# A fused mixer and mixture-of-experts layer: the first norm's weight and bias applied to gathered rows instead of stored rows, and both norms' vectors spread in the router's tail

## The chip, the core and the metric

One core of one Trainium2 chip. The metric is device time of one execution in microseconds (us), smaller is better. The kernel is written with Bass and Tile; TensorE (PE in the profile), VectorE (DVE), ScalarE (ACT), GpSimd (POOL) and SyncE (SP, which only issues DMAs) run side by side, and semaphores hold them together.

## What is computed

One layer on 1024 tokens of width 1024: a mixer (two kinds of gated linear attention, not touched here), a residual and a norm, a router that picks one of 8 groups and 2 of its 8 experts for each token, the 64 experts, a residual and a second norm.

```python
def layer_norm(x, g, b):
    ...
    return ((xf - mu) * lax.rsqrt(var + LN_EPS) * g + b).astype(x.dtype)

h = hybrid_mixer(x, ...)                       # ends with o @ w_out
x = layer_norm(DEEPNORM_ALPHA * x + h, ln1_g, ln1_b)
h = hierarchical_moe(x, ...)                   # router, top 2 of 64 experts, gates
x = layer_norm(DEEPNORM_ALPHA * x + h, ln2_g, ln2_b)

# inside hierarchical_moe, for the rows xb_ of one expert e
h = jax.nn.silu(xb_ @ w_gate[e]) * (xb_ @ w_up[e])
return h @ w_down[e]
```

Each expert has three weight matrices of 1024x512, 512x1024 in f32, 2 MB each.

## The kernel before

The program has three stages. The **mixer** runs to about 480 us. The **router stage** loops over eight tiles of 128 tokens (L952 to 979): output projection (L858 to 860), residual and statistics of norm 1 on VectorE (L868 to 885), the normalised row on ScalarE (`scaled_rows`, L894), its weight and bias on GpSimd (L896, L897, on the whole row for tiles 0 to 6; on tile 7 VectorE takes 704 columns and GpSimd 320), a store of the row to the DRAM array `x1d` (L898), and beside that the router's logits (transposes L908, matmuls L916, into which norm 1's weight and bias are already folded), the choice of experts (L763 to 808, VectorE with small ScalarE exponentials), and each token's rank within its expert (`ranks`: matmuls L814, L815, L840, with VectorE's L821 to L829). The tables of which token stands in which row of which expert (`gidx`, `oidx`, `gcol`; L982 to 987) close the stage.

The **expert stage** (`pairs`, from L1139) walks over 32 pairs of experts; 64 rows of each expert make one tile of 128 rows. A pair has six weight units of 2 MB (gate, up and down of both experts) that the SP queue loads into eight slots (`load_unit`, L719 on; tiles `w1u`, `w2u`). A slot is loaded anew as soon as the matmuls that read it are done. For a pair the order on TensorE is: 32 gate and up matmuls (L1156, 64 records), the rows' sums of an earlier pair (`add_rows`, L1114), the transposes of the hidden units (L1040), the transposes of the next pair's rows (`transposed`, L1024), and 16 down matmuls (L1182, 32 records); this order is written out by hand, the other engines' orders are set by the scheduler. The rows come through GpSimd's indirect DMA: `gather` (L1010) reads a pair's 128 rows of `x1d` into one of four buffers `xgs`, two pairs ahead of use. Once a pair's sums are known, VectorE adds the residual, which are those same gathered rows, in place and applies norm 2 to them (`finish_rows` L1117, L1123 and L1124; the norm L1054 to 1057, with rsqrt steps L80 to L88), and `scatter` (L1015) writes them to the output. A token has two experts; a row's norm is taken where both parts are known, and the indices of the others point outside the array.

In pair 0 `spread_ln2` (L1074 to 1084) makes copies of norm 2's weight and bias on all 128 partitions: `ident` times the vector's columns on VectorE (L1078), four matmuls by a matrix of ones (L1082, eight records), and ScalarE copies to SBUF. The buffers `xgs`, two for transposed rows (`xts`) and the two vectors share `VOA`, eight tiles of 128x1024 that the mixer used before. After the pairs a loop over overflow blocks follows for experts with more than 64 rows; it is counted at run time.

Of the kernel before, what the change touches and what calls it, by code (L numbers as in the profile page):

```python
# [9 lines left out]
F32 = mybir.dt.float32  # L10
# [3 lines left out]
AF = mybir.ActivationFunctionType  # L14
OP = mybir.AluOpType
# [4 lines left out]
D = 1024  # L20
NT = T // 128
KT = D // 128
NH = 8
NE = 64
# [32 lines left out]
def mixer_moe_kernel(ctx: ExitStack, tc: tile.TileContext, x_in, xT_in, wf_in, wv_in, wvg_in, wa2_in,  # L57
                     cols_in, wout_in, ln_in, wr_in, wg_in, wu_in, wd_in, const_in, out):
    nc = tc.nc
    npair = NE // 2  # L60
    V, S, G, PE = nc.vector, nc.scalar, nc.gpsimd, nc.tensor
# [640 lines left out]
    rp = b1.enter_context(tc.tile_pool(name="rp", bufs=2, reuse_waits="tile"))  # L702
    sp2 = b1.enter_context(tc.tile_pool(name="sp2", bufs=2, reuse_waits="tile"))
    wout_tiles(rp, [7])
    lnb = rp.tile([128, 2, D], F32, name="lnb", bufs=1)
    wr = rp.tile([128, KT, 72], F32, name="wr", bufs=1)
    load_wout(7, rp, D)
    for i in range(2):
        S.dma_start(lnb[:, i], ln_in[i:i + 1].to_broadcast([128, D]))
    S.dma_start(wr, wr_in)  # L710
    w1p = ctx.enter_context(tc.tile_pool(name="w1", bufs=W1N, side="right", reuse_waits="tile"))
    units = []
# [175 lines left out]
    def scaled_rows(t):  # L888

        r = rt[t]  # L890
        rs, nm, _ = stats[t]
        for n in range(2):
            ns = slice(n * 512, (n + 1) * 512)
            S.activation(r[:, ns], r[:, ns], AF.Identity, bias=nm, scale=rs)  # L894
        for E, cs in ((G, slice(0, D)),) if t < NT - 1 else ((V, slice(0, 704)), (G, slice(704, D))):
            E.tensor_tensor(r[:, cs], r[:, cs], lnb[:, 0, cs], OP.mult)  # L896
            E.tensor_tensor(r[:, cs], r[:, cs], lnb[:, 1, cs], OP.add)  # L897
        S.dma_start(x1d[t * 128:(t + 1) * 128], r)  # L898

    def logits(t):  # L900
# [51 lines left out]
    for t in range(NT):  # L952
# [20 lines left out]
        if t:  # L973
            scaled_rows(t - 1)
    scaled_rows(t)
    router(t)
    for u in (t - 1, t):
        ranks(u, stats[t][2])
# [16 lines left out]
    ps_c = mp.enter_context(tc.tile_pool(name="ps_c", bufs=2, space=PSUM))  # L995
    w2p = ctx.enter_context(tc.tile_pool(name="w2", bufs=W2N, reuse_waits="tile"))
    m1 = ctx.enter_context(tc.tile_pool(name="m1", bufs=1, reuse_waits="tile"))

    room = [VOA[:, i].rearrange("p h d -> p (h d)") for i in range(NT)]
    xgs, xts = room[:4], room[6:]  # L1000
    ln2 = VOA[:, 4:6].rearrange("p a h d -> p a (h d)")
    for xg in xgs[:2]:
        G.memset(xg, 0.0)
    mw = ctx.enter_context(tc.tile_pool(name="mw", bufs=2, reuse_waits="tile"))
# [4 lines left out]
    def gather(dst, idx):  # L1009
        return G.indirect_dma_start(out=dst, out_offset=None, in_=x1d,  # L1010
                             in_offset=bass.IndirectOffsetOnAxis(ap=idx, axis=0),
                             bounds_check=T - 1, oob_is_err=False)
# [2 lines left out]
        return G.indirect_dma_start(out=dst, out_offset=bass.IndirectOffsetOnAxis(ap=idx, axis=0),  # L1015
                             in_=src, in_offset=None, bounds_check=rows - 1, oob_is_err=False)

    def transposed(src, i):
        xt = xts[i].rearrange("p (c s) -> p c s", c=KT)
        sv = src.rearrange("p (k c) -> p c k", c=KT)  # L1020
        for half in range(2):
            tp = ps_x.tile([128, 4, 128], F32, name="tp")
            for i in range(4):
                PE.transpose(tp[:, i], sv[:, half * 4 + i], ident)  # L1024
            S.copy(xt[:, 4 * half:4 * half + 4], tp)
        return xt

    def product(gp, up):
# [22 lines left out]
    def norm2(o, stats_of, w):  # L1051

        mv = mw.tile([128, 2], F32, name="mv")
        V.bn_aggr(mv, stats_of.rearrange("p a b -> p (a b)"))  # L1054
        rs = rstd_of(mw, mv[:, 1:2], 1, "z")
        V.scalar_tensor_tensor(o, o, mv[:, 0:1], w[:, 0], op0=OP.subtract, op1=OP.mult)
        return V.scalar_tensor_tensor(o, o, rs, w[:, 1], op0=OP.mult, op1=OP.add)  # L1057

    over = m1.tile([128, 1], I32, name="over")
    onum = m1.tile([128, 1], I32, name="onum")  # L1060
# [10 lines left out]

    one1 = m1.tile([128, 1], F32, name="one1")

    def spread_ln2():  # L1074

        w = xgs[3]
        for i in range(2):
            V.tensor_tensor(w.rearrange("p (q c) -> p q c", c=8), ident[:, :, None].to_broadcast([128, 128, 8]),  # L1078
                            cols[:, None, 50 + 8 * i:58 + 8 * i].to_broadcast([128, 128, 8]), OP.mult)
            for n in range(2):  # L1080
                cp = ps_c.tile([128, 512], F32, name="cp")
                PE.matmul(cp, one1.to_broadcast([128, 128]), w[:, n * 512:(n + 1) * 512], start=True, stop=True)  # L1082
                S.copy(ln2[:, i, n * 512:(n + 1) * 512], cp)
        G.memset(w, 0.0)

    GP = 4

# [28 lines left out]

    def finish_rows(p, cps):  # L1117

        xg = xgs[p % 4]
        st = mw.tile([128, 2, 6], F32, name="st")  # L1120
        for n in range(2):
            ns = slice(n * 512, (n + 1) * 512)
            V.scalar_tensor_tensor(xg[:, ns], xg[:, ns], ALPHA, cps[n], op0=OP.mult, op1=OP.add)  # L1123
            V.bn_stats(st[:, n], xg[:, ns])  # L1124
        norm2(xg, st, ln2)
        outs.append(scatter(out, oidx[:, p:p + 1], xg, T))

    ys, outs = {}, []
    for p in range(2):
        g = gather(xgs[p], gidx[:, p:p + 1])  # L1130
        if p == 0:
            first = g
    G.memset(one1, 1.0)
    G.memset(xgs[2], 0.0)
    why = "the rows of the first pair go before weights that are needed later"
# [3 lines left out]
    def pairs():  # L1139


        wm = ps_c.tile([128, 128], F32, name="cp")
        for i in range(8):

            PE.matmul(wm, ident, ident, start=True, stop=True)
        last = npair - 1
        xt, cps, ms, trow = transposed(xgs[0], 0), None, None, None
        for p in range(npair):
            if p + 2 < npair:
                gather(xgs[(p + 2) % 4], gidx[:, p + 2:p + 3])  # L1150
            gp = ps_g.tile([128, FF], F32, name="gu")
            up = ps_g.tile([128, FF], F32, name="gu")
            for u, dst in ((0, gp), (2, up)):
                for c in range(KT):
                    for b in range(2):
                        PE.matmul(dst[64 * b:64 * b + 64], xt[:, c, 64 * b:64 * b + 64], utile[6 * p + u + b][:, c],  # L1156
                                  start=(c == 0), stop=(c == KT - 1))
                for b in range(2):
                    load_unit(6 * p + u + b + W1N + W2N)
            sg = product(gp, up)  # L1160
            if p:
                cps = [ps_c.tile([128, 512], F32, name="cp") for _ in range(2)]
                add_rows(cps, ms)
            hT = hidden(sg)
            if p:
                finish_rows(p - 1, cps)
            if p == 0:
                spread_ln2()
            if p < last:
                xt = transposed(xgs[(p + 1) % 4], (p + 1) % 2)  # L1170
            if p % GP == 0:
                trow = group_rows(p // GP)
            ms = masks(trow, p)
            if p == last:
                cps = [ps_g.tile([128, 512], F32, name="gu") for _ in range(2)]
                add_rows(cps, ms[:-1], last=False)
            yps = [ps_y.tile([128, 512], F32, name="yp") for _ in range(2)]
            ys[p] = yring.tile([128, 2, D], F32R, name="y")
            for n in range(2):
# [16 lines left out]
    def block_tables():  # L1196
# [20 lines left out]
        blk = cst[:, C_BLK:C_BLK + NOV]  # L1217
        ex = t1(NOV)
        for q in range(NOV // 16):
            cm = xts[q % 2].rearrange("p (a b) -> p a b", b=NE)  # L1220
            V.tensor_tensor(cm, inc[:, None, :].to_broadcast([128, 16, NE]),
                            blk[:, 16 * q:16 * q + 16, None].to_broadcast([128, 16, NE]), OP.is_le)
            V.tensor_reduce(ex[:, 16 * q:16 * q + 16], cm, AX.X, OP.add)
# [33 lines left out]
    def block(i):  # L1257
# [6 lines left out]
        V.tensor_copy(oc, ogate[:, bass.ds(i, 1)])  # L1264
        xo = xgs[0]
        gather(xo, oi[:, 0:1])
        xt = transposed(xo, 0)
        gp = ps_g.tile([128, FF], F32, name="gu")
        up = ps_g.tile([128, FF], F32, name="gu")
        for src, dst in ((wg_in, gp), (wu_in, up)):  # L1270
# [16 lines left out]
    def block_sums():  # L1287
        for t in range(NT):
            z, y0, y1 = xgs[0], xgs[1], xgs[2]
            ts = slice(t * 128, (t + 1) * 128)  # L1290
            nc.sync.dma_start(z, x1d[ts])
            nc.sync.dma_start(y0, yd[ts])
            nc.sync.dma_start(y1, yd[T + t * 128:T + (t + 1) * 128])
            V.tensor_tensor(y0, y0, y1, OP.add)
# [76 lines left out]
```

## Time and profile before

| | us |
|---|---|
| median of 3 runs | 1600.44 |
| lowest, highest | 1598.53, 1600.70 |
| the profiled execution | 1601.88 |
| its span in the profile | 1600.1 |

| engine | busy us | share of the span | instructions |
|---|---|---|---|
| PE | 1442.8 | 90% | 9303 |
| DVE | 730.9 | 46% | 1842 |
| ACT | 408.1 | 26% | 752 |
| POOL | 276.8 | 17% | 228 |

The page gives one execution. [...] A timeline row gives start, duration, engine, line, operation, output and input tile, count, and in brackets the engine's idle time before it with what ended it. A row of the waits sums those idle times. An f32 matmul of the program leaves two records, a transpose one.

### The profile page before, as it was taken

Reading aid. Unit: us, or ns where it says so; the run is one execution under the profiler, and the core shown is the slowest. Engines: PE = TensorE matmul, PEld = TensorE weight load, DVE = VectorE, ACT = ScalarE, POOL = GpSimd, SP = SyncE. Lnnn points to the kernel's source line nnn. Section 1 sums busy time; section 2 is a strip of 40 time slices with the busy share of each in tenths; the row PEclk is TensorE's granted clock in tenths of the full one; section 3 lists DMA queues with packets and bytes.
Section 4 is the critical chain, followed back from the end, with each engine's and each line's share of the span. In section 5 each row is a group of like instructions: output and inputs, shape, how many; then the busy total and the mean of one; then the engine's idle time right before and its main releaser. Section 6 shows DMA issues by size and latency. Waiting matters only on the chain. (4 is left out here: it accounts for less than half of the span.)

```text
span 1600.1 us, 22873 instructions
## 1 busy us (share of the span) xinstructions
PE 1442.8 (90%) x9303; PEld 798.1 (50%) x9303; DVE 730.9 (46%) x1842; ACT 408.1 (26%) x752; POOL 276.8 (17%) x228
## 2 busy tenths in 40 slices
PE   7999999899999987999889899889988989889985
PEld 5777678677777873343333233334333334333432
DVE  4657645667768993242233234224223323422424
ACT  5545544555533222111111101101111110110110
POOL 4524223323204441000000000000100000000000
PEclk8999999999999997999999999999999999998998
DMA  4101111010137246999999999999999999999992
GB/s 166 42 27 35 34 34 34 29 34 27 35 105 317 80 179 260 398 426 427 425 426 427 426 427 426 426 425 426 426 426 426 426 425 427 425 425 426 420 391 87
DMA packets 61966, 450.18 MB, mean 281 GB/s; under 512 B 12192, under 2 KB 20640, under 8 KB 36896
## 3 DMA queue, kind: packets, MB, share of 16 engines
q1 hardware_dynamic: 50768, 430.01, 64.7%
q0 software_dynamic: 9216, 12.61, 2.2%
q10 hardware_dynamic: 1872, 6.06, 1.0%
q8 instruction: 74, 1.21, 0.3%
q14 instruction: 36, 0.29, 0.1%
HBM read 448.63 MB, written 20.97 MB: 293 GB/s over the span
## 5 line engine op out<-in xcount | busy, mean ns | idle before, releaser
L1156 PE MATMUL gu<-w2u,VOA 128*64 128x512 f32 x1024 | 261.3, 639 | 45.4 <-DMA w2u<-in_wu_dram 28.4
L1156 PE MATMUL gu<-w1u,VOA 128*64 128x512 f32 x1024 | 259.8, 626 | 32.1 <-DMA w1u<-in_wu_dram 23.2
L1032 DVE TENSOR_TENSOR sg<-sg,gu 128x512 f32<-128x512 f32 x32 | 22.0, 687 | 542.8 <-PE gu L1156 542.8
L1156 PEld LDWEIGHTS gu<-w2u,VOA 128*64 128x64 f32 x1024 | 80.6, 147 | 215.3 <-issue 151.4
L1156 PEld LDWEIGHTS gu<-w1u,VOA 128*64 128x64 f32 x1024 | 82.5, 143 | 204.7 <-issue 152.7
L176 PE MATMUL pp<-xh,wh 128*128 128x512 f32 x416 | 173.1, 416 | 0.0
L178 PE MATMUL pp<-xl,wh 128*128 128x512 f32 x416 | 166.0, 399 | 0.0
L180 PE MATMUL pp<-xh,wl 128*128 128x512 f32 x416 | 165.0, 397 | 0.0
L1015 POOL DMA_INDIRECT out_dram<-VOA,oidx x32 | 32.2, 1005 | 604.7 <-DVE VOA L1057 592.9
L1042 ACT COPY hT<-tp 128x512 f32<-128x512 f32 x32 | 18.7, 585 | 386.4 <-PE tp L1040 386.4
L1182 PE MATMUL yp<-w1u,hT 128*64 128x512 f32 x512 | 117.2, 595 | 0.0
L1182 PE MATMUL yp<-w2u,hT 128*64 128x512 f32 x512 | 113.4, 595 | 0.0
L1048 ACT ACTIVATE y<-yp,gcol 128x512 fp32r<-128x512 f32 x64 | 44.0, 687 | 191.2 <-PE yp L1182 191.2
L176 PEld LDWEIGHTS pp<-xh,wh 128*128 128x128 f32 x416 | 79.0, 190 | 18.4 <-issue 1.9
L180 PEld LDWEIGHTS pp<-xh,wl 128*128 128x128 f32 x416 | 79.1, 190 | 17.3
L471 POOL TENSOR_TENSOR d<-P 128x512 f32<-128x512 f32 x36 | 51.6, 1433 | 202.3 <-DVE ny L88 65.3
L178 PEld LDWEIGHTS pp<-xl,wh 128*128 128x128 f32 x416 | 79.3, 191 | 13.7
L1010 POOL DMA_INDIRECT VOA<-x1d,gidx x32 | 32.7, 1021 | 292.6 <-issue 225.2
L1049 DVE SCALAR_TENSOR_TENSOR y<-yp,gcol,y 128x512 fp32r<-128x512 f32 x64 | 47.9, 749 | 77.4 <-ACT y L1048 77.1
L1031 ACT ACTIVATE sg<-gu 128x512 f32<-128x512 f32 x32 | 19.1, 597 | 246.7 <-PE gu L1156 246.7
L1114 PE MATMUL cp<-y,same 128*128 128x512 f32 x304 | 78.5, 404 | 0.0
L1114 PEld LDWEIGHTS cp<-y,same 128*128 128x128 f32 x304 | 54.7, 188 | 35.5 <-issue 25.2
(276 smaller groups left out, 2076.2 us busy)
## 6 DMA issues: line engine op xcount, KB each, us to landing
w1u<-in_wu_dram SPq DMA_DIRECT2D x32, 2048.0 KB, 29.5
w1u<-in_wd_dram SPq DMA_DIRECT2D x32, 2048.0 KB, 30.1
w2u<-in_wg_dram SPq DMA_DIRECT2D x31, 2048.0 KB, 26.8
w1u<-in_wg_dram SPq DMA_DIRECT2D x30, 2048.0 KB, 29.3
w2u<-in_wd_dram SPq DMA_DIRECT2D x30, 2048.0 KB, 30.4
w2u<-in_wu_dram SPq DMA_DIRECT2D x30, 2048.0 KB, 28.6
wr<-in_wf_dram SPq DMA_DIRECT2D x36, 256.0 KB, 2.6
r<-in_x_dram SPq DMA_DIRECT2D x8, 512.0 KB, 3.5
```

The source lines that it names most:

```text
L176: PE.matmul(ps, hi[:, k], xh[:, k, ts], start=(k == 0), stop=False)
L178: PE.matmul(ps, hi[:, k], xl[:, k, ts], start=False, stop=False)
L180: PE.matmul(ps, lo[:, k], xh[:, k, ts], start=False, stop=(k == KT - 1))
L471: G.tensor_tensor(ev[:, :, 0], ref, Pv[:, :, 0], OP.subtract)
L1010: return G.indirect_dma_start(out=dst, out_offset=None, in_=x1d, in_offset=bass.IndirectOffsetOnAxis(ap=idx, axis=0), bounds_check=T - 1, ...
L1015: return G.indirect_dma_start(out=dst, out_offset=bass.IndirectOffsetOnAxis(ap=idx, axis=0), in_=src, in_offset=None, bounds_check=rows - ...
L1032: V.tensor_tensor(sg, sg, up, OP.mult)
L1048: S.mul(yh[:, ns], yps[n], gate_col)
L1049: V.scalar_tensor_tensor(yl[:, ns], yps[n], gate_col, yh[:, ns], op0=OP.mult, op1=OP.subtract)
L1114: PE.matmul(cps[n], m, ys[q][:, i, n * 512:(n + 1) * 512], start=(first and j == 0 and i == 0), stop=(last and j == len(ms) - 1 and i == 1))
L1156: PE.matmul(dst[64 * b:64 * b + 64], xt[:, c, 64 * b:64 * b + 64], utile[6 * p + u + b][:, c], start=(c == 0), stop=(c == KT - 1))
L1182: PE.matmul(yps[n][64 * b:64 * b + 64], hT[:, c, 64 * b:64 * b + 64], utile[6 * p + 4 + b][:, c, n * 512:(n + 1) * 512], start=(c == 0), s ...
```

## The change

Rows are stored in `x1d` without norm 1's weight and bias. The tile `lnb` with its two broadcast loads goes, and so do lines 895 to 897. Four vectors (weight and bias of both norms) are spread over the partitions in the router's tail by 32 small matmuls (a column of `cols`, broadcast, times `ident`) and 8 ScalarE copies that write every eighth word; `spread_ln2` goes. The expert matmuls' operand gets weight and bias while ScalarE evicts the transposes, where they are a scale and a bias for each partition: eight activations of 128x128 instead of two copies of 128x512. The residual's rows get them by `gained`: two GpSimd operations of 128x1024 for each pair, in place. In the overflow blocks VectorE does this. `VOA` now holds three row buffers, four vectors and one buffer of transposed rows; a gather goes out one pair ahead instead of two.

```diff
-    lnb = rp.tile([128, 2, D], F32, name="lnb", bufs=1)
-    for i in range(2):
-        S.dma_start(lnb[:, i], ln_in[i:i + 1].to_broadcast([128, D]))
...
     def scaled_rows(t):
...
-        for E, cs in ((G, slice(0, D)),) if t < NT - 1 else ((V, slice(0, 704)), (G, slice(704, D))):
-            E.tensor_tensor(r[:, cs], r[:, cs], lnb[:, 0, cs], OP.mult)
-            E.tensor_tensor(r[:, cs], r[:, cs], lnb[:, 1, cs], OP.add)
         S.dma_start(x1d[t * 128:(t + 1) * 128], r)
...
     scaled_rows(t)
+    room = [VOA[:, i].rearrange("p h d -> p (h d)") for i in range(NT)]
+    xgs, lns, xts = room[:3], room[3:7], room[7]
+    ln1, ln2 = lns[:2], lns[2:]
+    for i, w in enumerate(lns):
+        for half in range(2):
+            tp = ps_h.tile([128, 4, 128], F32, name="hp")
+            for j in range(4):
+                c = 34 + 8 * i + 4 * half + j
+                PE.matmul(tp[:, j], cols[:, c:c + 1].to_broadcast([128, 128]), ident, start=True, stop=True)
+            S.copy(w.rearrange("p (q c) -> p c q", c=8)[:, 4 * half:4 * half + 4], tp)
     router(t)
...
-            S.copy(xt[:, 4 * half:4 * half + 4], tp)
+            for i in range(4):
+                c = half * 4 + i
+                S.activation(xt[:, c], tp[:, i], AF.Identity, bias=cols[:, 42 + c:43 + c], scale=cols[:, 34 + c:35 + c])
...
-    def spread_ln2():
...
+    def gained(E, o):
+
+        E.tensor_tensor(o, o, ln1[0], OP.mult)
+        E.tensor_tensor(o, o, ln1[1], OP.add)
...
-        xg = xgs[p % 4]
+        xg = xgs[p % 3]
...
-            if p + 2 < npair:
-                gather(xgs[(p + 2) % 4], gidx[:, p + 2:p + 3])
+            if p < last:
+                gather(xgs[(p + 1) % 3], gidx[:, p + 1:p + 2])
+            gained(G, xgs[p % 3])
...
-            if p == 0:
-                spread_ln2()
             if p < last:
-                xt = transposed(xgs[(p + 1) % 4], (p + 1) % 2)
+                xt = transposed(xgs[(p + 1) % 3])
```

How this moves instructions shows in three places. TensorE's order in the router's tail, before: logits of tile 7 (L908, L916), ranks of tiles 6 and 7 (L814, L815, L840; tile 7's are those behind the logits), the matmuls L1145 that keep the engine busy, then the first pair's transposes.

```order
L916 MATMUL hp<-wr,xt 128x72 x8
L814 LDWEIGHTS oneb
L814 MATMUL lp<-msb,oneb 128x64
L815 LDWEIGHTS trib
L815 MATMUL lp<-m,trib 128x64
L840 MATMUL tabp<-rhs,so 64x64 x8
L1145 MATMUL cp<-cst 128x128 x8
L1024 MATMUL tp<-cst,VOA 128x128 x8
```

The same place now, with the spreading matmuls at L979:

```order
L910 MATMUL hp<-wr,xt 128x72 x4
L979 MATMUL hp<-cst,cols 128x128
L910 MATMUL hp<-wr,xt 128x72 x4
L979 MATMUL hp<-cst,cols 128x128 x23
L837 MATMUL tabp<-rhs,so 64x64 x2
L979 MATMUL hp<-cst,cols 128x128 x8
L837 MATMUL tabp<-rhs,so 64x64 x2
L811 LDWEIGHTS oneb
L811 MATMUL lp<-msb,oneb 128x64
L812 LDWEIGHTS trib
L812 MATMUL lp<-m,trib 128x64
L837 MATMUL tabp<-rhs,so 64x64 x4
```

All 32 spreading matmuls stand ahead of the ranks' matmul of tile 7 (L812). ScalarE's order in the tail is now (the copies L980; L892 the store of tile 7's rows; L792 to L798 the softmax's exponentials of tile 7):

```order
L980 COPY VOA<-hp 128x4x128
L891 ACTIVATE r<-r,nm,rs 128x512 x2
L980 COPY VOA<-hp 128x4x128
L892 DMA x1d<-r 128x1024
L980 COPY VOA<-hp 128x4x128 x5
L792 ACTIVATE gs,gz<-gs 128x8
L980 COPY VOA<-hp 128x4x128
```

Seven of the eight copies stand ahead of the first exponential; before, nothing but the scaling of the rows (L894) stood there. GpSimd's order in the expert stage, which before alternated one gather (L1010) and one scatter (L1015), is now, from the first scatter on:

```order
L1016 DMA out_dram<-VOA,oidx 1024x1024
L1011 DMA VOA<-x1d,gidx 128x1024
L1080 TENSOR_TENSOR VOA<-VOA 128x1024
L1081 TENSOR_TENSOR VOA<-VOA 128x1024
L1016 DMA out_dram<-VOA,oidx 1024x1024
L1011 DMA VOA<-x1d,gidx 128x1024
```

Between a gather and the next scatter stand the two operations on the rows just gathered (L1080, L1081).

## Rows read from the trace of the kernel before

**Rows 1.** Windows: stretch; PE, PEld, DVE, ACT, POOL busy; PEclk, DMA share, GB/s.
```profile
580.00:620.00 40.00, 27.42 (x152) 22.06 (x152) 28.26 (x141) 10.05 (x26) 11.70 (x9) 0.74 0.63 229
700.00:1560.00 860.00, 775.46 (x3343) 304.07 (x3341) 269.60 (x695) 106.36 (x176) 55.65 (x55) 0.96 1.01 424
```

**Rows 2.** Waits of TensorE, 640 to 1560 us: us in total, times, longest.
```profile
PE gu L1156 <- DMA w2u<-in_wu_dram: 27.9, 13, 3.2
```

**Rows 3.** Timeline of PE (start, us, line): first transposes of three pairs.
```profile
663.05 0.62 PE L1024 MATMUL tp<-cst,VOA 128*128 128x128 f32 x4
...
687.76 0.62 PE L1024 MATMUL tp<-cst,VOA 128*128 128x128 f32 x4
...
1511.33 0.62 PE L1024 MATMUL tp<-cst,VOA 128*128 128x128 f32 x4
```

**Rows 4.** Timelines of POOL and, last row, DVE beside it, from 577 us.
```profile
577.14 2.36 POOL L896 TENSOR_TENSOR r<-r,lnb 128x1024 f32<-128x1024 f32 x1 [1.34 <-ACT r L894]
579.58 2.39 POOL L897 TENSOR_TENSOR r<-r,lnb 128x1024 f32<-128x1024 f32 x1
...
577.24 2.28 DVE L882 SCALAR_TENSOR_TENSOR nrs<-ge,nrs 128x1 f32<-128x1 f32 x1
```

**Rows 5.** Waits of TensorE, 480 to 596 us, columns as in rows 2.
```profile
PE lp L815 <- DVE m L787: 2.0, 1, 2.0
PE lp L916 <- DVE mv L871: 1.7, 4, 0.5
PE tabp L840 <- DVE ge L877: 1.0, 1, 1.0
```

**Rows 6.** Windows, columns as in rows 1, of three stretches of 5 us.
```profile
585.00:590.00 5.00, 4.51 (x25) 4.16 (x25) 2.71 (x20) 2.81 (x6) 0.65 (x1) 0.66 0.98 400
600.00:605.00 5.00, 2.81 (x14) 2.53 (x14) 4.45 (x25) 1.92 (x5) 1.33 (x2) 0.50 0.12 51
645.00:650.00 5.00, 5.00 (x26) 1.72 (x24) 1.50 (x2) 0.84 (x2) 0.00 (x0) 1.00 0.67 223
```

**Rows 7.** Timelines of DVE (two rows) and PE in the router's tail.
```profile
604.55 1.58 DVE L896 TENSOR_TENSOR r<-r,lnb 128x704 f32<-128x704 f32 x1
...
606.23 0.88 DVE L897 TENSOR_TENSOR r<-r,lnb 128x704 f32<-128x704 f32 x1
...
599.31 3.29 PE L916 MATMUL hp<-wr,xt 128*128 128x72 f32 x16
...
608.60 0.21 PE L815 MATMUL lp<-m,trib 128*128 128x64 bf16 x1 [5.26 <-DVE m L787]
...
612.54 3.75 PE L1145 MATMUL cp<-cst 128*128 128x128 f32 x16 [0.71 <-DVE gidx L984]
```

**Rows 8.** Copies: ACT's group by form; DVE's L462, L475 (ns min/median/max).
```profile
L1025 ACT COPY VOA<-tp 128x512 f32<-128x512 f32 x64 | 37.5, 589 | 18.3 <-PE tp L1024 18.3
...
L462 DVE TENSOR_TENSOR Qb<-q,d x6: 662/676/1068, 40.3 to 366.9; 128x512 f32<-128x512 f32 x6
...
L475 DVE TENSOR_TENSOR Qb<-q,d x36: 676/684/1750, 48.5 to 420.4; 128x512 f32<-128x512 f32 x36
```

**Rows 9.** Timeline of PE in pair 0.
```profile
633.29 1.88 PE L1082 MATMUL cp<-VOA,one 128*128 128x512 f32 x4
...
638.38 1.05 PE L1024 MATMUL tp<-cst,VOA 128*128 128x128 f32 x8
```

**Rows 10.** PE, POOL, DVE timelines, 959 to 967 us; POOL's waits; DMA landing.
```profile
959.82 0.61 PE L1024 MATMUL tp<-cst,VOA 128*128 128x128 f32 x4
...
966.28 1.01 POOL L1015 DMA_INDIRECT out_dram<-VOA,oidx  x1 [18.21 <-DVE VOA L1057]
...
964.71 1.28 DVE L1057 SCALAR_TENSOR_TENSOR VOA<-VOA,zy 128x1024 f32<-128x1024 f32 x1
...
POOL VOA L1010 <- issue: 224.6, 22, 11.2
...
VOA<-x1d,gidx POOLq DMA_INDIRECT x32, 10.5
```

More of the change, by code (lines that the diff above doesn't have):

```diff
@@ L997, in mixer_moe_kernel @@
     m1 = ctx.enter_context(tc.tile_pool(name="m1", bufs=1, reuse_waits="tile"))
-    room = [VOA[:, i].rearrange("p h d -> p (h d)") for i in range(NT)]
-    xgs, xts = room[:4], room[6:]
-    ln2 = VOA[:, 4:6].rearrange("p a h d -> p a (h d)")
     for xg in xgs[:2]:
@@ L1016, in scatter, with transposed @@
                              in_=src, in_offset=None, bounds_check=rows - 1, oob_is_err=False)
-    def transposed(src, i):
-        xt = xts[i].rearrange("p (c s) -> p c s", c=KT)
+    def transposed(src):
+        xt = xts.rearrange("p (c s) -> p c s", c=KT)
         sv = src.rearrange("p (k c) -> p c k", c=KT)
@@ L1055, in norm2 @@
         rs = rstd_of(mw, mv[:, 1:2], 1, "z")
-        V.scalar_tensor_tensor(o, o, mv[:, 0:1], w[:, 0], op0=OP.subtract, op1=OP.mult)
-        return V.scalar_tensor_tensor(o, o, rs, w[:, 1], op0=OP.mult, op1=OP.add)
+        V.scalar_tensor_tensor(o, o, mv[:, 0:1], w[0], op0=OP.subtract, op1=OP.mult)
+        return V.scalar_tensor_tensor(o, o, rs, w[1], op0=OP.mult, op1=OP.add)
     over = m1.tile([128, 1], I32, name="over")
@@ L1072, in mixer_moe_kernel @@
     one1 = m1.tile([128, 1], F32, name="one1")
-    def spread_ln2():
[L1076 to L1084, printed above, removed]
+    def gained(E, o):
+        E.tensor_tensor(o, o, ln1[0], OP.mult)
+        E.tensor_tensor(o, o, ln1[1], OP.add)
     GP = 4
@@ L1128, in mixer_moe_kernel @@
     ys, outs = {}, []
-    for p in range(2):
-        g = gather(xgs[p], gidx[:, p:p + 1])
-        if p == 0:
-            first = g
+    first = gather(xgs[0], gidx[:, 0:1])
     G.memset(one1, 1.0)
@@ L1146, in pairs @@
         last = npair - 1
-        xt, cps, ms, trow = transposed(xgs[0], 0), None, None, None
+        xt, cps, ms, trow = transposed(xgs[0]), None, None, None
         for p in range(npair):
-            if p + 2 < npair:
-                gather(xgs[(p + 2) % 4], gidx[:, p + 2:p + 3])
+            if p < last:
+                gather(xgs[(p + 1) % 3], gidx[:, p + 1:p + 2])
+            gained(G, xgs[p % 3])
             gp = ps_g.tile([128, FF], F32, name="gu")
@@ L1166, in pairs @@
                 finish_rows(p - 1, cps)
-            if p == 0:
-                spread_ln2()
             if p < last:
-                xt = transposed(xgs[(p + 1) % 4], (p + 1) % 2)
+                xt = transposed(xgs[(p + 1) % 3])
             if p % GP == 0:
@@ L1219, in block_tables @@
         for q in range(NOV // 16):
-            cm = xts[q % 2].rearrange("p (a b) -> p a b", b=NE)
+            cm = xts.rearrange("p (a b) -> p a b", b=NE)
             V.tensor_tensor(cm, inc[:, None, :].to_broadcast([128, 16, NE]),
@@ L1266, in block @@
         gather(xo, oi[:, 0:1])
-        xt = transposed(xo, 0)
+        xt = transposed(xo)
         gp = ps_g.tile([128, FF], F32, name="gu")
@@ L1293, in block_sums @@
             nc.sync.dma_start(y1, yd[T + t * 128:T + (t + 1) * 128])
+            gained(V, z)
             V.tensor_tensor(y0, y0, y1, OP.add)
```

## The prediction

> **What bounds the kernel now.** I read the windows of the trace first, stage by stage. From 700 to 1560 us the DMA share is 1.01 at 424 GB/s while TensorE is busy 775 of 860 us: the expert stage is fed by its weights and nothing else moves its end [rows 1]. Between 580 and 620 us it is the other way round: DMA share 0.63, TensorE 27 of 40 us, granted clock 0.74. There both are half idle, and a microsecond won is one by which all later weight transfers start sooner. The view of waits says the same: between 640 and 1560 us TensorE waits on weights, 13 times on one kind of unit alone, 27.9 us together and 3.2 at the longest [rows 2]. So work taken off the expert stage's engines pays nothing; what counts is how early that stage starts, whether the weight queue ever runs dry, and whether a new loop becomes longer than the weights' period. That period is read from the first transposes of the pairs: 663.05 to 1511.33 us are 28 periods, 30.30 us each. TensorE alone needs less: 663.05 to 687.76 us, in a stretch that waits for no weights, is 24.7; with the mean number of mask matmuls and the group rows about 25.4 [rows 3].
>
> **The change, part by part.** *The router stage.* Seven times GpSimd's two passes over 128x1024 go away. While they run, VectorE stands: an operation on one column that began beside the first took 2.28 us [rows 4]. The two passes last 577.14 to 581.97, 4.8 us, and the stall is felt on TensorE where VectorE comes late: in the waits of 480 to 596 us three entries name VectorE, 2.0, 1.7 (four small ones) and 1.0 us [rows 5]. The 2.0 is followed by a window of 5 us at a granted clock of 0.66, so 5 x 0.34 = 1.7 us of work is lost to the clock [rows 6]. I take 2.0 + 1.0 + 1.7 = **4.7 us** gained and keep the 1.7 of the four small waits, which hang on the length of VectorE's own chain, as the further bound. The two broadcast loads of the vectors go too; no wait in these stages names them, so they are worth nothing.
>
> *The router's tail.* Tile 7 loses VectorE's two operations of 1.58 and 0.88 us, 2.5 together, that stand before the ranks [rows 7]. It gains 32 matmuls of 128 columns on TensorE, all ahead of the ranks' matmul of tile 7 in the new order, and 8 copies on ScalarE. TensorE now waits 5.26 us before that matmul. [...] ScalarE's 8 copies take 0.589 each by the nearest row, a PSUM copy of 128x512, 4.7 us [rows 8]; some of these stand before the exponentials of tile 7, so the gates come no sooner than TensorE's part. 7.5 - 5.3 - 3 = -0.8; with some of the stretch at the low level I take **-0.5 us**. Ends: -2.5, if the whole of VectorE's saving shows, and +6.7 (9.7 - 3) with the matmuls at the low clock throughout.
>
> The copies write every eighth word. The trace has a row near it: an operation of VectorE that steps by two words on 128x512 has a median of 676 ns, one on halves of contiguous words 684 [rows 8], so step two costs nothing there. Step eight, and ScalarE, no row shows. [...] The sum stays with 0.589.
>
> *Pair 0.* The spreading of the second norm's vectors between pair 0's hidden units and the next transposes goes: its matmuls begin at 633.29, the transposes follow at 638.38 [rows 9]. Without it the transposes come about 4.7 us sooner and with them pair 0's down matmuls, which free two weight slots. The weight queue runs thin just then: 223 GB/s and a DMA share of 0.67 in 645 to 650 us [rows 6], so 5 x 0.33 = **1.6 us** of transfer time come back. Ends: 0 if the queue thins out at another place, 2.4 by the bytes (5 x (1 - 223/424)).
>
> *The transposes' eviction.* Eight activations of 128x128 replace two copies of 128x512. TensorE needs their result only at the next pair's gate matmuls, and this pair's down matmuls lie between. Nothing; if that cover were gone (it is, before pair 0 only), a few tenths either way.
>
> *The gain on GpSimd, and gathers one pair ahead.* This is the only added work in the stage that the weights bound, and it makes a new loop. With three row buffers, the gather of a pair must wait for the scatter that last used its buffer, which now happens only one pair before its rows are transposed. GpSimd's queue, in order, is: gather, multiply, add, scatter, next gather. The multiply waits for the transposes of its rows, so it starts just as VectorE works on the norm whose result the scatter takes. VectorE then stands for 4.8 us, as it did in the router stage [rows 4]. The loop, from one pair's transposes to the next's: scatter 6.5 us after the transposes (959.82 to 966.28), 4.8 of stall, scatter's issue to the next gather 11.2 (the 22 waits have a mean of 10.2, and the issue takes 1.0), gather's landing 10.5, 0.2 to the first transpose [rows 10]: 33.2 us. That is more than 30.30. But a pair whose transposes came late has its norm done by then, only the 4.8 us before its scatter remain, and the next loop is shorter. Late and timely pairs alternate: two pairs take one loop and one pair of TensorE's own, the latter with 1.7 us for the clock that falls after the wait [rows 6]: (33.2 + 25.4 + 1.7)/2 = 30.15 us a pair, against 30.30 for the weights. The loop nearly fills the period, so the two waits will not always fall together; I take 0.05 us a pair, x 28 = **+1.5 us**. Each microsecond on the loop above its spare 0.3 costs 14 us. The low end is 0. For the high end, GpSimd's multiply may itself have to wait for a VectorE operation under way; the norm's long ones take 1.28 us (L1057) [rows 10]. Then the loop is 34.5, the period 30.8, the cost 0.5 x 28 = 14 us.
>
> The rest, the gain in the overflow blocks and the masks' buffers, is in code that the chain of this run does not pass or moves no instruction.
>
> **Sum:** -4.7 - 0.5 - 1.6 + 1.5 = -5.3. The profiled execution took 1601.88 us, so 1596.6; the median of the runs shown is 1.44 lower: **1595.1 us**.
>
> **The rivals.** *B, the gather loop takes over.* It decides from a period of 30.3 us on, and outweighs the earlier start once the loop is 0.8 us longer than I made it. For it: the loop was summed at means, it holds two indirect transfers of 10 us on queues that share engines with the weights, and GpSimd may have to wait as VectorE does. Against: pairs alternate, and the longest of the 22 waits is just 1.0 above the mean. At 34.5 us: 1601.9 - 6.8 + 14 = 1609.1, as a median 1607.6. Slower.
> *C, the start is lost again in the tail.* 32 matmuls at the low clock (+6.7 in place of -0.5) give 1601.9 - 4.7 + 6.7 - 1.6 + 1.5 = 1603.8, median 1602.3; copies of twice 0.589, which also hold the four PSUM buffers that the matmuls fill, +4.7, give 1601.3, median 1599.8. For it: the window at 600 us shows 0.50 [rows 6]. [...] Against: the clock fell there in waits which the new matmuls fill. About the same time as before.
> *D, the loop hides wholly and the tail wins all of VectorE's time:* -4.7 - 1.7 - 2.5 - 2.4 = -11.3, median 1589.1. Against it: needs every bound at once. It is the low end of my forecast.
>
> **How the numbers follow.** About 0.2%, 3.2 us, is what a measurement of this kernel can tell from none. My forecast with D at its low end 0.55, of which 0.50 is faster and 0.05 the same; C 0.20, of which 0.17 the same and 0.03 slower; B 0.25, of which 0.21 slower and 0.04 the same (a loop only a few tenths too long). That makes faster 0.50, same 0.26, slower 0.24. The range goes from D to B, 1589 to 1608; half of B and a little of D lie outside.
>
> **What would show it.** Right: no VectorE operation of 2.3 us in the router stage; no wait of 2 us for VectorE before the ranks; the expert stage's first gate matmul some 5 us sooner; the 32 spreading matmuls near 0.24 us each; VectorE's norm operations stretched beside the GpSimd multiply; transposes that wait for gathered rows in alternate pairs, while the waits on weights shrink by about as much; periods of 30.3 still. Wrong: a period of 30.6 or more with weights no longer waited for (B); a granted clock of 0.50 through the spreading or copies of 1 us (C); transposes that wait for rows in every pair, which would mean that my alternation fails.

## The result, and the profile after

| | before | after |
|---|---|---|
| median of 4 runs, us | 1600.57 | 1591.71 |
| lowest, highest | 1598.53, 1602.27 | 1590.95, 1592.15 |
| the profiled execution | 1601.88 | 1590.95 |
| its span | 1600.1 | 1589.2 |

The ratio is 0.9946, 95% interval 0.9934 to 0.9958: 8.9 us faster, where 5.3 were forecast. A second measurement gave it again (1591.72 against 1601.06).

Three marks cut the stretch that changed: the first and the last output matmul of the router stage, and the first gate matmul. They stand in these rows of TensorE's timeline, first of before, then of after:

```profile
477.85 0.39 PE L858 MATMUL hp<-woh,oh 128*128 128x512 f32 x1
...
595.24 0.39 PE L860 MATMUL hp<-woh,ol 128*128 128x512 f32 x1
...
617.87 13.95 PE L1156 MATMUL gu<-w1u,VOA 128*64 128x512 f32 x64 [0.23 <-ACT VOA L1025]
```

```profile
476.04 0.39 PE L855 MATMUL hp<-woh,oh 128*128 128x512 f32 x1
...
586.32 0.39 PE L857 MATMUL hp<-woh,ol 128*128 128x512 f32 x1
...
608.98 13.95 PE L1151 MATMUL gu<-w1u,VOA 128*64 128x512 f32 x64 [0.17 <-ACT VOA L1029]
```

| stretch, us | before | after | difference | my term |
|---|---|---|---|---|
| start to first output matmul | 477.85 | 476.04 | -1.8 | none |
| to the end of the last output matmul | 117.78 | 110.67 | -7.1 | -4.7 |
| to the first gate matmul | 22.24 | 22.27 | 0.0 | -0.5 |
| to the end of the span | 982.2 | 980.2 | -2.0 | -1.6 + 1.5 |

The first line is code that the change does not touch. In the fourteen profiles of this study the first output matmul starts anywhere from 475.2 to 477.9 us from the start of the span, also for one and the same kernel (477.55 and 475.90), so it says which executions were profiled and nothing about the change. Without it the profiles differ by 9.1 us, the medians by 8.9.

**The router stage.** TensorE waited 4.7 us for VectorE before [rows 5]; after, the view of waits has no row for TensorE between 480 and 596 us. The stretch from the first to the last output matmul, as a window of before and then of after (columns as in [rows 1]: length of the window, then TensorE's busy time; PEclk is the granted share of TensorE's clock):

```profile
477.85:595.63 117.78, 113.15 (x609) 93.32 (x609) 104.46 (x376) 35.34 (x82) 55.13 (x31) 0.99 0.48 190
```

```profile
476.04:586.71 110.67, 110.66 (x609) 91.92 (x609) 74.00 (x386) 35.79 (x83) 20.97 (x17) 1.00 0.47 186
```

So 4.6 of the 7.1 us are idle time and 2.5 are busy time of the same 609 records, of which the window of low clock can account for 1.7. These windows of after answer to [rows 1] and [rows 6]:

```profile
580.00:620.00 40.00, 35.33 (x228) 25.39 (x229) 15.81 (x96) 17.16 (x34) 8.00 (x6) 0.91 0.71 262
700.00:1560.00 860.00, 768.41 (x3370) 313.50 (x3367) 352.10 (x701) 157.06 (x345) 199.34 (x112) 0.94 1.00 422
585.00:590.00 5.00, 4.85 (x41) 3.99 (x39) 4.59 (x22) 1.11 (x2) 0.10 (x1) 1.00 0.99 395
600.00:605.00 5.00, 2.24 (x15) 2.08 (x16) 2.51 (x15) 0.53 (x4) 1.20 (x1) 0.63 0.00 1
```

Windows go by time, and after is some 9 us further on in the program at 600 us. The fall of the clock to 0.66 at the end of the tiles' loop is gone; 0.63 from 600 us on goes with the waits for the gates and the first gather. From 700 us on the weights move as before, 422 GB/s, although GpSimd is busy 199 us there instead of 56 and VectorE 352 instead of 270: these are the two operations of `gained` and VectorE standing beside them.

**The tail.** It is as long as before, but of other parts. TensorE's and ScalarE's timelines of after:

```profile
590.42 5.48 PE L979 MATMUL hp<-cst,cols 128*128 128x128 f32 x46
...
598.38 0.19 PE L812 MATMUL lp<-m,trib 128*128 128x64 bf16 x1
602.05 0.70 PE L837 MATMUL tabp<-rhs,so 128*64 128x64 f32 x8 [3.48 <-DVE rhs L826]
```

```profile
591.34 1.09 ACT L980 COPY VOA<-hp 128x512 f32<-128x512 f32 x1 [2.51 <-PE hp L979]
...
594.47 4.85 ACT L980 COPY VOA<-hp 128x512 f32<-128x512 f32 x5
599.10 0.23 ACT L792 ACTIVATE gs<-gs 128x8 f32<-128x8 f32 x1
...
599.28 1.08 ACT L980 COPY VOA<-hp 128x512 f32<-128x512 f32 x1
600.13 0.23 ACT L795 ACTIVATE p<-p 128x2 f32<-128x2 f32 x1
```

46 records of the spreading matmuls in 5.48 us are 0.238 us for each matmul of two records, at a granted clock of 1.00 (590.42 to 595.90 us); in before 16 records of matmuls of the same size took 3.75 us [rows 7], 0.47 for two, at 0.50 (612.54 to 616.29 us). The ranks' matmul of tile 7 (L812) comes 11.7 us after the last output matmul, 13.0 before. Behind it TensorE waits 3.48 us for VectorE. VectorE's timeline says what held it:

```profile
598.46 0.26 DVE L821 TENSOR_SCALAR rhs<-oh,enc 128x64 f32<-128x64 bf16 x1 [3.78 <-PE tabp L837]
599.43 0.17 DVE L799 RECIPROCAL gz<-gz 128x1 f32<-128x1 f32 x1 [0.71 <-ACT gs L792]
...
600.56 0.16 DVE L800 RECIPROCAL ez<-ez 128x1 f32<-128x1 f32 x1 [0.34 <-ACT es L798]
```

It stood 3.78 us for a matmul of TensorE's ranks (L837) that stands behind the spreading matmuls, and then 0.71 and 0.34 us for ScalarE, where seven copies, about 1.0 us each, stand ahead of tile 7's exponentials. So the spreading holds the tail in two places: its matmuls ahead of the ranks, and its copies ahead of the exponentials.

**The expert stage.** Rows of the waits of TensorE after, from 635 to 1560 us, against [rows 2]:

```profile
PE tp L1026 <- DMA VOA<-x1d,gidx: 75.4, 23, 8.6
PE gu L1151 <- DMA w1u<-in_wu_dram: 8.2, 3, 3.1
PE gu L1151 <- DMA w2u<-in_wu_dram: 8.1, 5, 3.3
PE tp L1091 <- ACT VOA L1029: 6.7, 7, 1.2
```

The waits for weights have become waits for gathered rows, in 23 pairs. That GpSimd holds VectorE is seen where the prediction put it; timelines of GpSimd, VectorE and TensorE for one pair, against [rows 10]:

```profile
924.97 2.36 POOL L1080 TENSOR_TENSOR VOA<-VOA 128x1024 f32<-128x1024 f32 x1 [10.52 <-PE tp L1026]
...
931.97 1.04 POOL L1016 DMA_INDIRECT out_dram<-VOA,oidx  x1 [2.20 <-DVE VOA L1061]
942.61 1.01 POOL L1011 DMA_INDIRECT VOA<-x1d,gidx  x1 [9.60 <-DMA out_dram<-VOA,oidx]
...
925.07 2.28 DVE L86 TENSOR_TENSOR zt<-zy 128x1 f32<-128x1 f32 x1
...
927.57 2.21 DVE L88 SCALAR_TENSOR_TENSOR zy<-zt,zy 128x1 f32<-128x1 f32 x1
...
923.72 1.16 PE L1026 MATMUL tp<-cst,VOA 128*128 128x128 f32 x8 [2.74 <-DMA VOA<-x1d,gidx]
...
953.06 1.97 PE L1026 MATMUL tp<-cst,VOA 128*128 128x128 f32 x8 [4.00 <-DMA VOA<-x1d,gidx]
```

From transposes to transposes 29.3 us: 8.3 to the scatter, 10.6 to the next gather, 10.4 to the transposes. The two one-column operations of VectorE beside the multiply and the add took 2.28 and 2.21 us, where the median of the 96 of either line is 0.16 us.

### The profile page after: what moved, and what is told of

Same layout as the page of the kernel before. It is cut to its first block, busy times and chain, and to the rows that moved or that the text cites. A ratio compares the mean times of both kernels' runs of the same rounds, so it can differ in the third digit from the quotient of the medians.

```text
span 1589.2 us, 23253 instructions
## 1 busy us (share of the span) xinstructions
PE 1428.5 (90%) x9359; PEld 806.1 (51%) x9359; DVE 782.0 (49%) x1838; ACT 470.5 (30%) x948; POOL 401.7 (25%) x275
## 5 line engine op out<-in xcount | busy, mean ns | idle before, releaser
L1151 PE MATMUL gu<-w1u,VOA 128*64 128x512 f32 x1024 | 237.1, 606 | 8.7 <-DMA w1u<-in_wu_dram 8.2
L1151 PE MATMUL gu<-w2u,VOA 128*64 128x512 f32 x1024 | 232.6, 599 | 8.1 <-DMA w2u<-in_wu_dram 8.1
L1080 POOL TENSOR_TENSOR VOA<-VOA 128x1024 f32<-128x1024 f32 x32 | 81.1, 2534 | 368.4 <-PE tp L1026 367.0
L1151 PEld LDWEIGHTS gu<-w2u,VOA 128*64 128x64 f32 x1024 | 77.0, 139 | 157.8 <-issue 143.1
L1175 PE MATMUL yp<-w1u,hT 128*64 128x512 f32 x512 | 127.7, 656 | 0.0
L1175 PE MATMUL yp<-w2u,hT 128*64 128x512 f32 x512 | 122.2, 633 | 0.0
L1029 ACT ACTIVATE VOA<-tp,cols 128x128 f32<-128x128 f32 x256 | 93.0, 470 | 89.9 <-PE tp L1026 89.9
L1026 PE MATMUL tp<-cst,VOA 128*128 128x128 f32 x256 | 46.2, 330 | 77.6 <-DMA VOA<-x1d,gidx 75.5
L1081 POOL TENSOR_TENSOR VOA<-VOA 128x1024 f32<-128x1024 f32 x32 | 79.6, 2489 | 2.5
```

What stands on the lines that cost most here:

```text
L1029: S.activation(xt[:, c], tp[:, i], AF.Identity, bias=cols[:, 42 + c:43 + c], scale=cols[:, 34 + c:35 + c])
L1080: E.tensor_tensor(o, o, ln1[0], OP.mult)
L1081: E.tensor_tensor(o, o, ln1[1], OP.add)
```

## The experiments

My theory after the result: the gain is the router stage's, since GpSimd's passes held VectorE and VectorE held TensorE; pair 0 adds some 2 us; the gather loop costs next to nothing; and the spreading eats what the tail should have won. The rivals: the expert stage made the gain, or the loop hides a cost. In the table, ratios are to the kernel before on the same chip; "loop", "tail" and "experts" are the three stretches of the table above, from each run's profile. "Ranks" is the part of the tail from the end of the last output matmul to the ranks' matmul of tile 7 (L815 of before, L812 of after).

| run | median us | ratio, 95% interval | loop | ranks | tail | experts |
|---|---|---|---|---|---|---|
| before | 1600.57 | | 117.8 | 13.0 | 22.2 | 982.2 |
| the change | 1591.71 | 0.9946, 0.9934 to 0.9958 | 110.7 | 11.7 | 22.3 | 980.2 |
| after_again | 1591.72 | 0.9941, 0.9927 to 0.9955 | 110.7 | 11.7 | 22.1 | 980.2 |
| e1_no_router_passes | 1587.05 | 0.9922, 0.9908 to 0.9935 | 110.7 | 7.6 | 16.0 | 982.6 |
| e1_again | 1588.95 | 0.9921, 0.9908 to 0.9934 | 110.8 | 7.6 | 16.7 | 982.4 |
| e2_no_gain_op | 1590.99 | 0.9945, 0.9931 to 0.9958 | 110.7 | 11.7 | 22.0 | 980.4 |
| e3_pool_program_order | 1591.63 | 0.9942, 0.9928 to 0.9956 | 110.7 | 11.7 | 21.8 | 980.1 |
| e4_copies_runs_of_4 | 1589.54 | 0.9928, 0.9914 to 0.9941 | 110.7 | 11.5 | 21.0 | 980.1 |
| e5_no_pair0_spread | 1596.50 | 0.9970, 0.9958 to 0.9982 | 118.3 | 10.0 | 19.7 | 980.2 |
| e9_vectors_by_dma | 1584.69 | 0.9903, 0.9887 to 0.9918 | 110.7 | 7.6 | 16.0 | 980.3 |
| e10_dma_and_program_order | 1584.90 | 0.9902, 0.9889 to 0.9915 | 110.7 | 7.6 | 16.6 | 980.4 |
| e11_gain_twice_as_long | 1699.66 | 1.0616, 1.0597 to 1.0635 | 110.7 | 11.7 | 22.2 | 1088.0 |
| e12_spread_after_ranks | 1586.14 | 0.9916, 0.9903 to 0.9929 | 110.7 | 8.8 | 17.2 | 980.1 |
| e13_no_passes_no_pair0 | 1586.16 | 0.9914, 0.9897 to 0.9930 | 111.0 | 7.6 | 16.1 | 979.0 |

Of one and the same tail the profiles differ by up to 0.7 us (16.0 and 16.7 in the two runs of e1), behind the ranks' matmul; up to it they agree within 0.1 us.

**after_again.** No edit.

> The change itself, once more on the chip of the next three, as their measure. 8 to 9 us under the kernel before, as first measured (1591.7 against 1600.6).

It came out so, 9.3 us under before.

**e1_no_router_passes.** From the kernel before:

```diff
-        for E, cs in ((G, slice(0, D)),) if t < NT - 1 else ((V, slice(0, 704)), (G, slice(704, D))):
-            E.tensor_tensor(r[:, cs], r[:, cs], lnb[:, 0, cs], OP.mult)
-            E.tensor_tensor(r[:, cs], r[:, cs], lnb[:, 1, cs], OP.add)
```

> The kernel before, without the two passes that put norm 1's weight and bias on the rows in the router stage (left out; gathered rows stay without them). My theory: these passes hold VectorE and with it TensorE, 7 us in the loop over the tiles; in the tail VectorE's 2.5 us come on top as far as they show, since nothing is spread there: 7 to 9.6 us under before, 1591 to 1593.5, TensorE without waits for VectorE between 480 and 590 us. Rival: the router stage gave only the 4.7 us that I summed, and the rest of the change's gain comes from the expert stage (pair 0, order of gathers): 4.7 to 5.5 under before, 1595 to 1596.

The loop over tiles is as short as in the change, so those 7.1 us are the passes' alone, as the theory had it. The tail was a miss: 6.2 us shorter, not 2.5 at most, and the median 14 us under before on the same chip. Its timeline of TensorE (the ranks' matmul now waits 0.77 us where it waited 5.26 [rows 7]):

```profile
588.29 2.00 PE L913 MATMUL hp<-wr,xt 128*128 128x72 f32 x16
...
594.24 0.21 PE L815 MATMUL lp<-m,trib 128*128 128x64 bf16 x1 [0.77 <-DVE m L787]
...
602.67 1.51 PE L1153 MATMUL gu<-w1u,VOA 128*64 128x512 f32 x6 [0.23 <-ACT VOA L1022]
```

The tail before held more than tile 7's own operations. VectorE was late from tile 6's passes: its first residual of tile 7 (L868) began 0.4 us after the end of the last output matmul, here 2.4 us before that end. VectorE's rows of before and of e1:

```profile
596.04 0.69 DVE L868 SCALAR_TENSOR_TENSOR r<-r,hp 128x512 f32<-128x512 f32 x1
```

```profile
584.28 0.68 DVE L868 SCALAR_TENSOR_TENSOR r<-r,hp 128x512 f32<-128x512 f32 x1
```

And tile 7's logits (16 records, which are eight matmuls) took 3.29 us [rows 7] at a granted clock of 0.54 (599.31 to 602.60 us), here 2.00; in after the same 16, with two spreading records among them, took 2.23 us at 1.00 (588.36 to 590.59 us). So the passes cost 13.3 us in all, 7.1 and 6.2; the change pays 6.2 of that for the spreading and gains 2.0 in the expert stage. The repeat, on another chip:

> The kernel before without the router stage's passes once more, on the chip of the next three, as the measure of the third. 12 to 14 us under before, as first measured.

It is 11 us under before by the medians, less than expected, and 12.6 by the ratio; the first run's ratio gives 12.5.

**e2_no_gain_op and e3_pool_program_order.** The loop's cost, measured by taking its two operations away, and by moving them behind the next gather:

```diff
-            gained(G, xgs[p % 3])
```

```diff
-    with tc.manual_schedule(engines={mybir.EngineType.PE}):
+    with tc.manual_schedule(engines={mybir.EngineType.PE, mybir.EngineType.Pool}):
         pairs()
```

> The change without GpSimd's multiply and add in the expert stage (the residual's rows stay without norm 1's weight and bias). Theory: the gather loop sits just at the weights' period and costs 1 us or less; waits for gathered rows fall from 75 us to under 20, waits for weights come back to 60 to 80, time 0 to 1.5 us under the change. Rival: the three buffers and the shorter lead are the limit and not the two operations: waits for rows stay over 40 us. Rival: the loop costs the 3 us or more that the other end of my bounds would make: time 3 us or more under the change.

> The change with GpSimd's expert stage in program order: the multiply and add of a pair come after the gather of the next pair is issued, not before the scatter of the pair ahead. Theory: they then fall into time in which VectorE has no norm, the scatter no longer waits for them, the loop shrinks by up to 4.8 us to about 28.4, waits for rows fall under 20 us, and the time is that of the run without the two operations, 0 to 1.5 us under the change. Rival (the stall just moves to another VectorE operation that TensorE waits for): time as the change or above, with waits of TensorE for VectorE or ScalarE in the expert stage.

Neither is faster than the change beyond the interval, and the expert stage is 980.1 to 980.4 us long in all three. The loop costs nothing that can be measured. In e2 the waits for rows fell to 26.7 us (my bound was 20), those for weights rose to 56. In e3 the waits of TensorE from 620 us on were:

```profile
PE gu L1151 <- DMA w2u<-in_wu_dram: 35.2, 13, 3.3
PE gu L1151 <- DMA w1u<-in_wu_dram: 20.4, 10, 3.3
PE tp L1026 <- DMA VOA<-x1d,gidx: 16.9, 7, 4.1
```

So the 75 us of waits for rows in the change are waits that would otherwise be for weights. A wait's length says who came last, not what it costs.

**e11_gain_twice_as_long.** How near to the edge the loop lies: two passes more.

```diff
         E.tensor_tensor(o, o, ln1[1], OP.add)
+        for op in (OP.subtract, OP.add) if E is G else ():
+            E.tensor_tensor(o, o, ln1[1], op)
```

> The change with two more passes on GpSimd in each pair (the bias taken off and put on again), so the stretch in which VectorE stands and the scatter waits is 9.7 us instead of 4.8. Theory: the gather loop of the change lies just at the weights' period; with 4.8 more it must show. Of a late pair: transposes 1.6, passes 9.7, scatter to next gather 11.1, landing 10.5, 0.2: 33.1 us against 30.4, over 28 pairs +75 us: 1660 to 1670, waits for weights near zero, waits for rows over 150 us. Rival (the loop has slack which my sum does not see, since the scatter could overtake or the gathers are not what the transposes wait for): under 1600.

1699.66 us, 108 above the change, where I expected 70 to 80. The loop is there and bounds the stage once it is longer than the weights' period; its size I had too small. A late pair is near the sum of 33.1 (961.17 - 927.74 = 33.4 us):

```profile
927.74 1.95 PE L1026 MATMUL tp<-cst,VOA 128*128 128x128 f32 x8 [5.69 <-DMA VOA<-x1d,gidx]
961.17 1.97 PE L1026 MATMUL tp<-cst,VOA 128*128 128x128 f32 x8 [6.86 <-DMA VOA<-x1d,gidx]
```

TensorE's waits for rows, from 635 to 1560 us:

```profile
PE tp L1026 <- DMA VOA<-x1d,gidx: 171.0, 26, 11.0
```

About every fourth period was near 36 us, which the sum does not hold; why, I did not take apart. No wait for weights is left.

**e4_copies_runs_of_4.** The copies' stride alone:

```diff
-            S.copy(w.rearrange("p (q c) -> p c q", c=8)[:, 4 * half:4 * half + 4], tp)
+            S.copy(w.rearrange("p (q c) -> p q c", c=8)[:, :, 4 * half:4 * half + 4], tp.rearrange("p c q -> p q c"))
```

> The change with its 8 spreading copies walked in the other order, so that each writes runs of four adjacent words instead of single words 32 bytes apart; same data. In the change's trace one takes 1.0 us, not the 0.589 that I had taken from contiguous copies, and 7 of them stand before the exponentials that the gates of tile 7 need. [...]

My estimate was copies of about 0.6 us, exponentials 2.5 to 3 us sooner, a tail of 20 +- 0.7 us and a time 1.5 to 2.5 us under the change. The rival: PSUM read in single words costs what writing single words would, or the matmuls set the end, and tail and time stay as in the change. ScalarE's group of the copies, first in the change, then in this run (in the change's the mean holds some overlap of neighbours, 7.8 us are busy for eight):

```profile
L980 ACT COPY VOA<-hp 128x512 f32<-128x512 f32 x8 | 7.8, 1122 | 2.5 <-PE hp L979 2.5
```

```profile
L980 ACT COPY VOA<-hp 128x512 f32<-128x512 f32 x8 | 4.5, 585 | 3.8 <-PE hp L979 3.6
```

The write of single words was the price; PSUM read in single words cost nothing (585 ns here, 589 for the contiguous copies of before [rows 8]). The tail fell by 1.1 to 1.3 us against the two runs of the change, less than I expected. The exponentials come 1.5 us sooner after the last output matmul, 10.9 us instead of 12.4, not 2.5 to 3, since ScalarE now waits more for the spreading matmuls (3.6 us of idle time instead of 2.5). And in the chain up to the gates VectorE now waits for TensorE alone, with the ranks' matmuls still behind the spreading ones:

```profile
600.02 0.25 DVE L821 TENSOR_SCALAR rhs<-oh,enc 128x64 f32<-128x64 bf16 x1 [3.65 <-PE tabp L837]
```

The intervals of this run and the change overlap, so the gain in time is shown by the stretch and not by the medians.

**e12_spread_after_ranks.** The whole spreading with the copies of e4, written behind `ranks` and `tables` in the program; the scheduler places it from there:

```diff
+    router(t)
+    for u in (t - 1, t):
+        ranks(u, stats[t][2])
+        tables(u)
     for i, w in enumerate(lns):
...
-    router(t)
-    for u in (t - 1, t):
-        ranks(u, stats[t][2])
-        tables(u)
```

> The change with the spreading (copies in runs of four) written after the ranks and tables, so that the scheduler puts seven of the eight copies behind the exponentials of tile 7 and the matmuls into TensorE's waits. Theory: not the work but its place ahead of the ranks and exponentials costs the 6 us; TensorE's waits between the last output matmul and the first gate matmul hold most of the 7.5 us: stretch 17 to 18.5 us, 3.5 to 5 us under the change. Rival: the work as such costs (copies hold PSUM, or the first transposes wait behind them): stretch 20 us or more, under 2 us below the change.

17.2 us, 1.2 above e9, whose tail spreads nothing. The same 32 matmuls and eight copies cost 5.0 us in e4, ahead of the ranks and the exponentials, and 1.2 here. The edit moves both, the matmuls on TensorE and the copies on ScalarE, so it does not say by itself which of them counts; of the 3.8 us between the two tails, 2.7 lie up to the ranks' matmul, which now comes 8.8 us after the last output matmul instead of 11.5.

**e9_vectors_by_dma.** The spreading replaced by loads (all four vectors are handed in as rows):

```diff
-        for half in range(2):
-            tp = ps_h.tile([128, 4, 128], F32, name="hp")
-            for j in range(4):
-                c = 34 + 8 * i + 4 * half + j
-                PE.matmul(tp[:, j], cols[:, c:c + 1].to_broadcast([128, 128]), ident, start=True, stop=True)
-            S.copy(w.rearrange("p (q c) -> p c q", c=8)[:, 4 * half:4 * half + 4], tp)
+        S.dma_start(w, ln_in[i:i + 1].to_broadcast([128, D]))
```

> The change with its 32 matmuls and 8 copies taken out and the four vectors brought in by four broadcast loads of 512 KB each on ScalarE's queue, into the same buffers as soon as the mixer's tiles there are used up. Theory: the spreading costs 6.1 us of the router's tail (22.1 us against 16.0 in the run without router passes), the loads run while the weight slots are full and cost nothing: stretch 16.0 to 16.5, time 5 to 6.5 us under the change, 1585 to 1586.5, and under the run without router passes by what pair 0 gives. Rival: 2 MB more on the DMA engines push the weights back by 2.0/0.425 = 4.9 us: 0 to 2 us under the change.

The best of all: 1584.69 us, ratio 0.9903, 7.0 us under the change by the medians (6.1 by the stretches) and 16 under before, with nothing left out. The tail is 16.0 us, and the ranks' matmul comes 7.6 us after the last output matmul, as in e1:

```profile
593.47 0.21 PE L812 MATMUL lp<-m,trib 128*128 128x64 bf16 x1 [0.77 <-DVE m L784]
```

The loads do not meet the weights: SyncE issues no weight unit between 489 and 576 us, and the share of the DMA engines is 0.31 from 515 to 575 us. That window, and two of the four issues in ScalarE's timeline:

```profile
515.00:575.00 60.00, 60.00 (x344) 49.99 (x344) 40.81 (x234) 18.48 (x46) 10.33 (x8) 1.00 0.31 114
```

```profile
541.78 0.33 ACTq L975 DMA_DIRECT2D VOA<-in_ln_dram  x1
...
556.09 0.34 ACTq L975 DMA_DIRECT2D VOA<-in_ln_dram  x1
```

**e10_dma_and_program_order.** That and e3's edit together.

> The run with the four vectors by DMA, with GpSimd's expert stage in program order besides. Theory: as after the change, the order moves waits from rows to weights and not the end, which the weights set: within 1.5 us of that run, ratio to before 0.989 to 0.9915, waits for rows under 25 us instead of 72. Rival: with the start 7 us sooner the loop was what held it: 2 us or more under that run, ratio under 0.989.

The same time, with waits for rows down from 71.7 to 18.1 us: also after a tail some 6 us shorter the weights set the end.

**e5_no_pair0_spread and e13_no_passes_no_pair0.** Pair 0's part, once from the kernel before and once from e1:

```diff
-            if p == 0:
-                spread_ln2()
```

> The kernel before without spread_ln2 (norm 2 then works with what lies in that buffer). Theory: TensorE reaches the first transposes of pair 0 5 us sooner, but the weights set the pace later on, so only the gap of the weight queue near 645 us counts: 0.5 to 2 us under before. Rival A: all 5 us are kept (the slots come free sooner for good): 4 to 5 us under. Rival B: nothing, since the queue then thins out elsewhere: within 0.4 us of before.

> The kernel before without the router stage's passes and without spread_ln2: pair 0's part by itself on top of the third run's measure, where the scheduler moves little else. Theory: 2 to 3 us under the run without the passes, by the gap of the weight queue (209 GB/s for 5 us, 5 x (1 - 209/425) = 2.5); the 4.5 us of the earlier run without spread_ln2 held 2.1 us that the router stage was shorter by. Rival: 4 to 5 us here too.

e5's 4.45 us looked like the rival's, but the table takes them apart: loop and tail are 2.0 us shorter together in it, where the order of VectorE's work in the router stage has changed too; the expert stage is 2.0 us shorter. The gap of the weight queue (223 GB/s in 645 to 650 us [rows 6]) is gone in e5:

```profile
640.00:650.00 10.00, 10.00 (x48) 3.30 (x46) 0.60 (x1) 0.60 (x1) 0.00 (x0) 1.00 1.01 430
```

In e13 the expert stage is 3.4 us shorter than in e1_again, by medians 2.8, though those intervals overlap. Over all runs the expert stage takes 982.2 to 982.6 us with `spread_ln2` and 979.0 to 980.4 without (e11 aside): about 2 us, of 5.1 us by which TensorE reaches the transposes of pair 0 sooner (624.40 - 608.98 = 15.4 us after the first gate matmul, against 20.5).

## Why the prediction was right

The direction, the place and the range were right; the size was 5.3 of 8.9 us. One term, the tail's, came out by luck, and one of my signs of being wrong, copies of 1 us, was there.

- *Router stage, -4.7: 7.1.* Right mechanism, mis-sized. I took the two large waits and one window of low clock (0.66) and kept the four small waits (1.7 us) as a bound, as "the length of VectorE's own chain". With the passes gone, no wait at all was left: they were the same cause. With them the term would have been 6.4; the last 0.7 I did not trace.
- *Tail, -0.5: 0.0.* Luck: two errors that cancel. The passes' removal is worth 6.2 us there (e1), where I counted 3 for earlier logits and had VectorE's 2.5 only in the low end; the spreading takes 6.1 to 6.3 of them (e9 against the two runs of the change). The step that failed is the cover: I let 7.5 us of spreading matmuls fill the 5.26 us for which TensorE waited ahead of the ranks' matmul. That wait belonged to the passes. Without them 3.2 us in three waits are left (0.77 of them at that matmul), and the matmuls, busy for 7.97 us in all at a granted clock of 1.00, make the ranks 4.1 us later (11.7 us after the last output matmul against 7.6 in e9). No run shows the sum's 7.5 us for these matmuls, the 9.7 of its end at the low clock, or its 3 us for tile 7's logits; what the runs showed in their place is the 7.97 us, a clock of 1.00 from the last output matmul to the ranks' matmul, and logits of 2.00 us instead of 3.29 (e1). The other 2 us lie behind the ranks' matmul, and 1.1 to 1.3 of the whole are rival C's second kind, copies of 1.0 us and not 0.589 (e4). There I had taken a contiguous copy as the nearest row, with the step-two row for support; eight copies were busy for 7.8 us, where eight of 0.589 are 4.7. The exponentials behind the copies I saw in ScalarE's new order and priced only as covered by TensorE.
- *Pair 0, -1.6: about -2.* Right, between the two ways of counting the gap (1.6 by share, 2.4 by bytes).
- *Eviction, nothing.* Nothing that shows in time: the expert stage is 980.2 us long in the change, 980.2 in e5 and 979.0 in e13, which both keep the two copies. But ScalarE's group of the eight activations in after has 93.0 us for 32 pairs, 2.9 a pair, against 37.5 for the copies [rows 8], and in 7 pairs the group rows' matmuls wait up to 1.2 us for them:

```profile
L1029 ACT ACTIVATE VOA<-tp,cols 128x128 f32<-128x128 f32 x256 | 93.0, 470 | 89.9 <-PE tp L1026 89.9
```

- *Gather loop, +1.5: 0.* The loop exists (e11), it lies at the weights' period, and the waits changed from weights to rows, as forecast. The alternation of late and timely pairs, from which I worked out the term, did not come: 23 of the pairs waited, eleven of them 2 to 4 us, so that VectorE's norm was partly done in the wait (in the pair shown, the scatter comes 8.3 us after the transposes, where I had summed 11.3). The first periods apart, they lay between 27 and 34 us.
- *Rivals.* B needed the loop to be 0.8 us longer than summed and did not happen, though e11 shows that 4.8 us more cost 108. Of C, the low clock did not come (1.00 through the spreading) and the slow copies did, at 1.1 to 1.3 us instead of the 4.7 that C put on them.

## What to carry over

An operation that holds another engine costs what waits behind that engine (the router stage's passes 13.3 us), so small waits with the same releaser belong to the same term; and a tail's worth is found by removing the whole cause, not by adding up the operations in it. A wait that the change itself takes away can't also cover the work that the change adds. One-time work belongs where no chain runs through its engine: the same spreading cost 5.0 us ahead of the ranks and the exponentials, 1.2 placed among and behind them, and nothing that shows as a DMA in a stretch in which no weights were loading. When two loops have nearly the same period, the view of waits shows only which came last; the price of either is known only once one is taken away or lengthened.

## What the runs showed that I had not expected

- ScalarE, copying 128x512 from PSUM to SBUF, took about 1.0 us (7.8 us for eight) where it wrote single words 32 bytes apart and 0.585 us in runs of four words; reading PSUM in single words was free (the contiguous copies of before took 0.589).
- An activation with a bias and a scale for each partition on 128x128 from PSUM took 470 ns in the mean; neighbours overlap, and eight of them took 2.9 us, two and a half times the two copies of 0.589 that they replace.
- The stretch before the first output matmul, the same code in all kernels, varied by 2.6 us between profiled executions. Differences of profiles below that are read from stretches and not from spans.
